# A decoder block on one core: the FFN's second product by seven half-size products, with weight sums made by DMA

## The chip, the core and the metric

The kernel runs on one core of one Trainium2 chip. A core has TensorE (PE, matmuls, with PEld for its weight loads), VectorE (DVE), ScalarE (ACT), GpSimd (POOL) and SyncE (SP, which here only issues DMAs), an on-chip memory SBUF of 128 partitions, a matmul accumulator PSUM of eight banks, and sixteen DMA engines to DRAM. The metric is the device time of one execution in microseconds, as the median of several runs; lower is better.

## The reference

One layer of a hybrid decoder: three mixers, their gated merge, an output projection, and a SwiGLU FFN, each half with an RMSNorm before and after and a residual. Batch 1, sequence S = 512, width D = 1024, FFN width DFF = 2816, all fp32. The changed part is the end:

```python
    x = x + rms_norm(merged @ w_out, norm_g[1])
    h = rms_norm(x, norm_g[2])
    gt, up = jnp.split(h @ w_ffn_in, 2, axis=-1)
    x = x + rms_norm((jax.nn.silu(gt) * up) @ w_ffn_out, norm_g[3])
```

## The kernel before

Every fp32 product is made of three fp32r matmuls (`mm3`, L119 to L122): high part by high part, high by low, low by high. A weight streams in as pieces of 128 x 1024 fp32 (512 KB): SP issues the load into `wraw` (three buffers), ACT casts it to `whi` (L92), and DVE or POOL subtracts to get `wlo` (L93); `whi` and `wlo` also have three buffers each. During the long projections a helper `take` keeps three pieces ahead of PE. The words "to split a tile" below mean these two operations, one on ACT and one on DVE or POOL.

The end of the kernel has three stages. The **front of the FFN** (L1176 to L1262): the output projection (w_out, eight pieces; 256 columns wide, so 384 matmuls of 256 columns) for token blocks 0 and 1 together and then 2 and 3 alone; behind each block `out_norm` (two squares on ACT, two multiplies by the gain on DVE, a reciprocal root, the residual `yf`, a square, another reciprocal root, `mix`), and `transpose_split` (L214 to L223), which turns `mix` by eight PE transposes and splits it into `hh` and `hl`. The first two column chunks of the FFN's first product go in `part` calls of 24 matmuls in that front, so that PE has work while the last blocks are normalised. The **first product** (`gemm_t`, L155 to L165) then goes chunk by chunk; `ffn_act` makes silu(gate) * up and splits it into `ah` and `al`. The **second product** (L1283 to L1331): 22 pieces of w_ffn_out, two passes of eleven (left and right half of the columns) into eight PSUM banks `acc`, four token blocks a pass, 24 matmuls of 512 columns for a piece, 528 in all. In the second pass the last three pieces are used block by block, so that a block's norm (square, gain, reciprocal root in `rstd_of`, residual, store) follows while PE is at the next block.

Each engine runs its own instructions in order. In this part of the kernel a scheduler has set that order. Splits in the FFN alternate between DVE and POOL (`cfg["lo"] = "vg"`, L1170).

## Time and profile before

| | us |
|---|---|
| median of three runs (range) | 1236.82 (1236.24 to 1239.58) |
| profiled execution | 1240.05 |
| its span in the trace | 1238.1 |
| PE busy in it | 1214.9 (98%) |
| DVE, ACT, POOL busy | 603.4, 526.7, 209.9 |
| front of the FFN, first w_out matmul to the first matmul of `gemm_t` | 815.21 to 892.07 |
| second product, first to last matmul | 1110.7 to 1230.3 |

An engine's busy time is the time in which it worked at something that the profiler records; the chain of waits follows the work that ended last back to the start. The page's own lines and the answers to queries on the trace stand in the section of rows below.

### The profile page before, as it was taken

What the parts mean: (1) busy time and instruction counts of PE and PEld (TensorE: products, weight loads), DVE (VectorE), ACT (ScalarE), POOL (GpSimd) and SP (SyncE); (2) the same over time, 40 slices, a digit from 0 to 9 for tenths busy, and PEclk for the clock granted to TensorE, in tenths of its full rate; (3) what the DMA queues carried; (4) which work ended last, traced back from release to release, by engine and by line L of the source; (5) the groups of instructions that cost most, each with busy time, mean ns of one, the idle gap of its engine ahead of it and who ended that gap; (6) DMA issues with size and microseconds to landing.
All of it is one profiled execution on the core that took longest, in us unless ns stands there. A gap on an engine that the chain in (4) does not pass through costs nothing.

```text
span 1238.1 us, 18045 instructions
## 1 busy us (share of the span) xinstructions
PE 1214.9 (98%) x7068; PEld 1032.8 (83%) x7068; DVE 603.4 (49%) x1275; ACT 526.7 (43%) x1008; POOL 209.9 (17%) x134
## 2 busy tenths in 40 slices
PE   8999999999999999999999999999999999999997
PEld 6887888787788888999998888898988888878886
DVE  6516657566576778465543343447433333331114
ACT  5335556665486676352432232334323222322222
POOL 1224544555000000000000000001122122221220
PEclk9998999999999999999999999999999999999999
DMA  7821422221233324223223343352233333322321
GB/s 254 236 73 36 88 70 65 65 65 52 67 104 96 94 68 108 83 70 82 73 69 102 92 145 121 102 171 69 58 97 102 102 99 89 102 90 98 94 94 68
DMA packets 152387, 117.99 MB, mean 95 GB/s; under 512 B 25106, under 2 KB 142078, under 8 KB 152304
## 3 DMA queue, kind: packets, MB, share of 16 engines
q1 hardware_dynamic: 151712, 115.81, 32.5%
q8 instruction: 55, 0.90, 0.3%
q10 hardware_dynamic: 592, 1.05, 0.2%
q14 instruction: 28, 0.23, 0.1%
HBM read 114.67 MB, written 2.17 MB: 94 GB/s over the span
## 4 chain that ended last, share of the span: by engine, by line
PE 90%; DVE 5%; ACT 3%; issue 1%; DMA 1%; SPq 0%; DVEq 0%; ACTq 0%
PE gps L797 17%; PE gps L162 13%; PE gps L800 9%; PE gps L120 7%; PE gps L165 7%; PE gps L121 7%; PE gps L122 7%; PE ops L650 3%; PE acc L120 3%; PE acc L121 3%; PE acc L122 3%; PE s L587 3%; PE ptp L627 2%; PE hid L426 1%; ACT p L598 1%
## 5 line engine op out<-in xcount | busy, mean ns | idle before, releaser
L92 ACT CAST whi<-wraw 128x1024 fp32r<-128x1024 f32 x177 | 185.0, 1050 | 350.3 <-PE gps L165 137.3
L93 DVE TENSOR_TENSOR wlo<-wraw,whi 128x1024 fp32r<-128x1024 f32 x122 | 148.9, 1228 | 242.6 <-ACT whi L92 165.8
L93 POOL TENSOR_TENSOR wlo<-wraw,whi 128x1024 fp32r<-128x1024 f32 x55 | 131.5, 2391 | 701.5 <-ACT whi L92 522.6
L162 PE MATMUL gps<-hh,whi 128*128 128x512 f32 x368 | 143.5, 390 | 0.0
L165 PE MATMUL gps<-hl,whi 128*128 128x512 f32 x368 | 143.4, 390 | 0.0
L797 PE MATMUL gps<-hh,whi 128*128 128x512 f32 x320 | 125.4, 392 | 1.5 <-ACT whi L92 1.5
L800 PE MATMUL gps<-hl,whi 128*128 128x512 f32 x320 | 124.6, 389 | 0.0
L605 POOL TENSOR_TENSOR p<-p,sc 128x256 f32<-128x256 f32 (+3 forms) x64 | 75.5, 1200 | 117.8 <-DVE sc L601 117.8
L120 PE MATMUL gps<-whi,hh 128*128 128x256 f32 x320 | 92.4, 289 | 0.0
L121 PE MATMUL gps<-wlo,hh 128*128 128x256 f32 x320 | 90.6, 283 | 1.5 <-DVE wlo L93 1.5
L162 PE MATMUL gps<-hh,wlo 128*128 128x512 f32 x368 | 90.9, 389 | 0.0
L122 PE MATMUL gps<-whi,hl 128*128 128x256 f32 x320 | 90.5, 283 | 0.0
L120 PE MATMUL gps<-hh,whi 128*128 128x512 f32 (+1 forms) x200 | 82.0, 415 | 3.4 <-ACT hh L222 1.5
L598 ACT ACTIVATE p<-p,mx 128x384 f32<-128x384 f32 (+3 forms) x128 | 68.7, 538 | 34.2 <-DVE mx L596 33.9
L162 PEld LDWEIGHTS gps<-hh,whi 128*128 128x128 f32 x368 | 69.1, 188 | 15.0 <-issue 0.9
L165 PEld LDWEIGHTS gps<-hl,whi 128*128 128x128 f32 x368 | 69.1, 188 | 14.5 <-issue 0.2
L162 PEld LDWEIGHTS gps<-hh,wlo 128*128 128x128 f32 x368 | 69.1, 188 | 14.4
L797 PE MATMUL gps<-hh,wlo 128*128 128x512 f32 x320 | 79.0, 389 | 0.0
L797 PE MATMUL gps<-yh,whi 128*128 128x512 f32 x192 | 74.9, 390 | 0.0
L800 PE MATMUL gps<-yl,whi 128*128 128x512 f32 x192 | 74.8, 389 | 0.0
L121 PE MATMUL gps<-hl,whi 128*128 128x512 f32 (+1 forms) x200 | 74.5, 374 | 0.0
L122 PE MATMUL gps<-hh,wlo 128*128 128x512 f32 (+1 forms) x200 | 74.2, 372 | 0.0
(314 smaller groups left out, 2401.9 us busy)
## 6 DMA issues: line engine op xcount, KB each, us to landing
wraw<-in_w_in_dram SPq DMA_DIRECT2D x60, 512.0 KB, 3.7
wraw<-in_w_ffn_in_dram SPq DMA_DIRECT2D x88, 256.0 KB, 3.2
wraw<-in_w_ffn_out_dram SPq DMA_DIRECT2D x22, 512.0 KB, 3.7
wraw<-in_w_in_dram SPq DMA_DIRECT2D x32, 256.0 KB, 3.2
wraw<-in_w_branch_dram SPq DMA_DIRECT2D x16, 512.0 KB, 3.3
bias<-line_d SPq DMA_DIRECT2D x16, 256.0 KB, 4.4
wraw<-in_w_in_dram SPq DMA_DIRECT2D x32, 128.0 KB, 2.7
wraw<-in_w_branch_dram SPq DMA_DIRECT2D x16, 256.0 KB, 4.4
```

Of the source, the lines that this page charges most:

```text
L92: a_.copy(hi, raw)
L93: lo_eng.tensor_tensor(lo, raw, f(hi), op=OP.subtract)
L120: pe.matmul(ps, lh, rh, start=first, stop=False)
L121: pe.matmul(ps, lh, rl, start=False, stop=False)
L122: pe.matmul(ps, ll, rh, start=False, stop=last)
L162: pe.matmul(ps[n], part_[:, k, c], ah[:, kk], start=kk == 0 and part_ is h, stop=kk == 7 and part_ is l)
L165: pe.matmul(ps[n], h[:, k, c], al[:, kk], start=False, stop=False)
L587: pe.matmul(s[gi][:, :n], q[h, qp, qs], kk[h, sl], start=i == 0, stop=i == 2)
L598: a_.activation(o, o, AF.Exp, scale=-1.0, bias=mx[:, br, gi:gi + 1], accum_out=sm[:, br, gi:gi + 1])
L605: g_.tensor_tensor(o, o, sc[:, br][:, :, None].to_broadcast([128, 2, n]), op=OP.mult)
L797: pe.matmul(ps[n], part_[:, k, c], ah[:, kk], start=kk == 0 and part_ is h, stop=kk == 7 and part_ is l)
L800: pe.matmul(ps[n], h[:, k, c], al[:, kk], start=False, stop=False)
```

## The change

**The second product.** The activations act (512 x 2816) and w_ffn_out (2816 x 1024) are cut in two in each dimension, and the four result quarters come from seven products of half size (p1 to p7) of sums and differences of quarters, instead of eight. A half-size product has 11 k steps (`NK`), two token tiles and three fp32r matmuls of 512 columns: 66 matmuls, 462 for seven. The first pass goes through k = 0 to 10 and uses two weight tiles at each: `tile_a` (two 256 KB loads) for p2 and p5, `tile_b` (one 256 KB load and a subtract on DVE) for p3 and p1. The second pass makes p4, p6 and p7 one after the other, six tiles each. So 40 tiles are split instead of 22, all on ACT and DVE. Each activation chunk pair becomes `ls` tiles by `first_sums`, `second_sums` and `split_ls`, and the result `C` lies in the old space of `hl`; adds and subtracts from the PSUM banks into C (`add`) are new. DVE, ACT and PE run this part in the order in which it is written.

**The weight sums.** Two tables in DRAM, `rows_d` and `cols_d`, hold sums of quarters of w_ffn_out. POOL issues 44 DMAs of 512 KB, DRAM to DRAM: 22 plain copies and 22 that accumulate onto them. Each follows a `tick`, a one-column copy on POOL that reads the `whi` tile of one of the pieces 12 to 55 of the projections, and so is paced by that stream.

**The front of the FFN.** w_out comes in pieces 512 columns wide (192 matmuls of 512 columns); the norms are cut in halves, those of blocks 0 and 1 run together; the pieces of the first two FFN chunks are split in the front and the `part` calls are all 256 tokens wide; the transposes (`turn`) stand at fixed places; x1 is also stored to DRAM (`x1_d`) and read back as `xr` before the last residual. POOL no longer splits FFN tiles.

The core of the diff:

```diff
+    def weight_sum(i, hi):
+        add, t, r, n, c0, c1, w = sums[i]
+        g_.tensor_copy(tick, f(hi[:, 0, 0:1]))
+        src = dap(w_ffn_out, r * D + (c1 if add else c0), [[D, n], [1, w]])
+        if add:
+            g_.dma_start(t[r:r + n], src, accum_op=OP.add, max_dma_last_dim=4096)
+        else:
+            g_.dma_start(t[r:r + n], src)
+
     def take():
         i = used[0]
         used[0] += 1
         while len(ready) < min(i + 3, len(pieces)):
-            ready.append(pieces[len(ready)]())
+            n = len(ready)
+            ready.append(pieces[n]())
+            if 12 <= n < 12 + len(sums):
+                weight_sum(n - 12, ready[n][0])
         return ready[i]
...
-    cfg["lo"] = "vg"
...
+        part(pss[0], fw[0], 0, t0, True, False)
+        turn(2)
+        s3 = norm_x((3,), s3)
+        norm_out((3,), s3)
+        part(pss[0], fw[1], 1, t0, False, False)
+        part(pss[1], fw[2], 0, t0, True, False)
+        part(pss[1], fw[3], 1, t0, False, False)
+        turn(3)
+        part(pss[0], fw[0], 0, t1, False, False)
...
+        def gain(tb, hf):
+
+            c = C[tb][:, hf * 512:hf * 512 + 512]
+            jk = fp.tile([128, 512], F32, name="fjk", tag="fsg", bufs=2)
+            a_.activation(jk, c, AF.Square, accum_out=ssf[:, tb, hf:hf + 1])
+            v_.tensor_tensor(c, c, gb3[:, hf * 512:hf * 512 + 512], op=OP.mult)
...
+            for k in range(NK):
+                w = weights()
+                use(p2, LS1[k], 1, w, 0, k)
+                use(p5, LS1[k], 2, w, 1, k)
...
+                w = weights()
+                use(p3, LS1[k], 3, w, 0, k)
+                use(p1, LS1[k], 0, w, 1, k)
...
+                if k:
+                    second(k - 1)
...
+            for p in range(NP - 3):
+                w = weights()
+                for k in range(2 * p, 2 * p + 2):
+                    use(p7, LS2[k], 1, w, k % 2, k)
+                if p in (0, 1):
+                    add(C[2 + p][:, c1], p6[p], C[2 + p][:, c1])
+                    gain(2 + p, 1)
+                    mean(2 + p)
+                if p == 1:
+                    root(2)
+                if p == 2:
+                    store(2, 0)
+                    store(2, 1)
+                    root(3)
+            w3 = [weights() for _ in range(3)]
+            for tt in range(2):
+                for k in range(2 * NP - 6, NK):
+                    use(p7, LS2[k], 1, w3[(k - 2 * NP + 6) // 2], k % 2, k, (tt,))
...
+            store(0, 0)
+            store(0, 1)
+            root(1)
+            store(1, 0)
+            store(1, 1)
```

`weights` takes the next split tile and has three split ahead (`ahead`); `mean` makes the mean square and its Sqrt on ACT, `root` the reciprocal and its correction on DVE, `store` the residual on DVE and the store of half a block, by ACT's queue for the left half and SP's for the right one.

**Order of ACT in the last product.** Before, behind the last pieces of the second pass (`whi_10520` to `whi_10532` are the last three; `fjk` is a block's square, `rs_r` its Sqrt):

```order
L92 CAST whi_10520<-wraw_10518 128x1024
L92 CAST whi_10526<-wraw_10524 128x1024
L92 CAST whi_10532<-wraw_10530 128x1024
L1307 ACTIVATE fjk_10554,ssf_9931<-acc10_9936 128x512
L202 ACT_TABLE_LOAD
L202 ACTIVATE rs_r_10562<-rs_m_10561 128x1
L1307 ACTIVATE fjk_10592,ssf_9931<-acc11_9937 128x512
```

After, in p7 (`whi_10633`, `whi_10662`, `whi_10696` and `whi_10723` are its third to sixth tile, the last of them half as wide):

```order
L1419 CAST whi_10633<-wraw_10630 128x1024
L1500 ACTIVATE fjk_10650,ssf_9815<-hl_9903 128x512
L1508 ACT_TABLE_LOAD
L1508 ACTIVATE rs_r_10656<-rs_m_10655 128x1
L1419 CAST whi_10662<-wraw_10659 128x1024
L1500 ACTIVATE fjk_10679,ssf_9815<-hl_9903 128x512
L1508 ACTIVATE rs_r_10685<-rs_m_10684 128x1
L1419 CAST whi_10696<-am_10693 128x1024
L1523 DMA out_0_dram<-hl_9903 128x512
L1419 CAST whi_10723<-am_10721 128x512
```

The squares and roots of blocks 2 and 3, which had stood behind the last split, now stand between the splits of the last three tiles.

**Order of DVE there.** Before, the last two subtracts and the first block's norm behind them (`fo` is the block's result):

```order
L93 TENSOR_TENSOR wlo_10521<-wraw_10518,whi_10520 128x1024
L93 TENSOR_TENSOR wlo_10533<-wraw_10530,whi_10532 128x1024
L1325 TENSOR_TENSOR fo_10557<-acc10_9936,gb3_9929 128x512
L1326 TENSOR_TENSOR ss3_10556<-ssf_9931 128x1
L201 TENSOR_SCALAR rs_m_10561<-ss3_10556 128x1
```

After, from the subtract of p7's fourth tile (`hl<-acc7` is the add of p6 into block 3, `rs_r_10656` block 2's root, `xr4` and `xr5` its residual):

```order
L1420 TENSOR_TENSOR wlo_10663<-wraw_10659,whi_10662 128x1024
L1551 TENSOR_TENSOR hl_9903<-acc7_9914,hl_9903 128x512
L1501 TENSOR_TENSOR hl_9903<-hl_9903,gb3_9813 128x512
L1505 TENSOR_TENSOR ss3_10682<-ssf_9815 128x1
L1507 TENSOR_SCALAR rs_m_10684<-ss3_10682 128x1
L1514 RECIPROCAL rs_r_10656<-rs_r_10656 128x1
L1515 SCALAR_TENSOR_TENSOR rs_t_10688<-rs_r_10656,rs_m_10655 128x1
L1516 TENSOR_SCALAR rs_t_10688<-rs_t_10688 128x1
L1517 TENSOR_TENSOR rs_r_10656<-rs_r_10656,rs_t_10688 128x1
L1420 TENSOR_TENSOR wlo_10697<-am_10693,whi_10696 128x1024
L1522 SCALAR_TENSOR_TENSOR hl_9903<-hl_9903,rs_r_10656,xr4_10492 128x512
L1522 SCALAR_TENSOR_TENSOR hl_9903<-hl_9903,rs_r_10656,xr5_10494 128x512
```

Block 3's add, gain and mean and block 2's root stand ahead of the fifth tile's subtract, and block 2's residual ahead of the sixth tile's.

**Order of POOL in the projections.** Before, POOL had little between the mixers' masks and the FFN (`p1`, `p2` are mixer tiles, `wlo_8311` belongs to the front of the FFN):

```order
L605 TENSOR_TENSOR p1_3673<-p1_3673,sc_3677 128x2x384
L605 TENSOR_TENSOR p2_3674<-p2_3674,sc_3677 128x768
L1117 AFFINE_SELECT cb_5008<-cb_5008 128x128
L1120 MEMSET at0_5009 128x512
L1120 MEMSET at1_5010 128x512
L93 TENSOR_TENSOR wlo_8311<-wraw_8307,whi_8310 128x1024
```

After, in the middle of the sums, where the plain copies end and the accumulating ones begin:

```order
L794 COPY tick_3871<-whi_5453 128x1
L799 DMA cols_d_101<-in_w_ffn_out_dram 256x512
L794 COPY tick_3871<-whi_5485 128x1
L799 DMA cols_d_101<-in_w_ffn_out_dram 256x512
L794 COPY tick_3871<-whi_5553 128x1
L797 DMA rows_d_100<-in_w_ffn_out_dram 128x1024
L794 COPY tick_3871<-whi_5611 128x1
L797 DMA rows_d_100<-in_w_ffn_out_dram 128x1024
```

A tick reads a `whi` buffer, so ACT's cast into that buffer, three pieces later, now waits for POOL to have come past that tick.

## Rows read from the trace of the kernel before

**Rows 1.** page: an engine's busy time and instructions; the chain of waits by engine
```profile
PE 1214.9 (98%) x7068; PEld 1032.8 (83%) x7068; DVE 603.4 (49%) x1275; ACT 526.7 (43%) x1008; POOL 209.9 (17%) x134
...
PE 90%; DVE 5%; ACT 3%; issue 1%; DMA 1%; SPq 0%; DVEq 0%; ACTq 0%
```

**Rows 2.** windows: busy time (count) of PE, PEld, DVE, ACT, POOL; clock, DMA, GB/s
```profile
650.00:700.00 50.00, 50.00 (x226) 41.52 (x225) 16.88 (x18) 13.98 (x17) 0.00 (x0) 1.00 0.33 95
...
1150.00:1200.00 50.00, 50.00 (x223) 41.39 (x222) 8.20 (x8) 12.36 (x18) 10.34 (x5) 1.00 0.32 97
```

**Rows 3.** tile `acc`: min/median/max ns, first and last start
```profile
L120 PE MATMUL acc<-whi,ah x176: 389/389/504, 1110.7 to 1229.9; 128*128 128x512 f32 x176
...
L122 PE MATMUL acc<-whi,al x176: 387/389/396, 1111.3 to 1230.3; 128*128 128x512 f32 x176
```

**Rows 4.** groups by line and form: busy, mean ns, idle before and releaser
```profile
L120 PE MATMUL acc<-whi,ah 128*128 128x512 f32 x176 | 68.6, 390 | 0.9 <-DVE fsg L1278 0.9
...
L92 ACT CAST whi<-wraw 128x1024 fp32r<-128x1024 f32 x177 | 185.0, 1050 | 350.3 <-PE gps L165 137.3 <-PE acc L122 79.2 <-PE gps L800 55.6
...
L93 DVE TENSOR_TENSOR wlo<-wraw,whi 128x1024 fp32r<-128x1024 f32 x122 | 148.9, 1228 | 242.6 <-ACT whi L92 165.8 <-PE gps L162 48.2 <-PE gps L797 23.2
...
L93 POOL TENSOR_TENSOR wlo<-wraw,whi 128x1024 fp32r<-128x1024 f32 x55 | 131.5, 2391 | 701.5 <-ACT whi L92 522.6 <-PE gps L162 177.4 <-DVE rs_r L203 1.5
...
L1215 DVE SCALAR_TENSOR_TENSOR yf<-mix,rs_r,yf 128x1024 f32<-128x1024 f32 x4 | 5.1, 1285 | 0.1
...
L1330 DVE SCALAR_TENSOR_TENSOR fo<-fo,rs_r,yf 128x512 f32<-128x512 f32 x8 | 5.7, 748 | 0.1
...
L202 ACT ACT_TABLE_LOAD x6 | 7.7, 1283 | 0.1
```

**Rows 5.** timeline of PE over the front of the FFN: start, length, instruction
```profile
815.21 0.28 PE L120 MATMUL gps<-whi,mth 128*128 128x256 f32 x1
...
861.18 1.03 PE L219 MATMUL tps<-ident,mix 128*128 128x128 f32 x8
...
863.49 0.61 PE L120 MATMUL gps<-hh,whi 128*128 128x256 f32 x3 [1.27 <-ACT hh L222]
...
865.20 0.38 PE L120 MATMUL gps<-hh,whi 128*128 128x256 f32 x1 [1.09 <-DVE mix L1211]
...
892.07 0.39 PE L162 MATMUL gps<-hh,whi 128*128 128x512 f32 x1
```

**Rows 6.** windows of the front: two around its longest PE wait
```profile
862.00:866.00 4.00, 1.42 (x8) 0.81 (x6) 3.59 (x9) 1.74 (x5) 0.00 (x0) 0.95 0.60 173
...
866.00:870.00 4.00, 4.00 (x24) 4.00 (x24) 2.40 (x9) 1.27 (x3) 0.00 (x0) 0.62 0.02 4
```

**Rows 7.** timeline of the end: PE, ACT and DVE
```profile
1230.31 0.39 PE L122 MATMUL acc<-whi,al 128*128 128x512 f32 x1
...
1230.80 0.60 ACT L1307 ACTIVATE fjk<-acc 128x512 f32<-128x512 f32 x1 [2.18 <-PE acc L122]
...
1231.52 0.69 DVE L1325 TENSOR_TENSOR fo<-acc,gb 128x512 f32<-128x512 f32 x1 [0.61 <-ACT fjk L1307]
...
1232.73 0.17 DVE L203 RECIPROCAL rs_r<-rs_r 128x1 f32<-128x1 f32 x1 [0.27 <-ACT rs_r L202]
...
1233.57 1.41 DVE L1330 SCALAR_TENSOR_TENSOR fo<-fo,rs_r,yf 128x512 f32<-128x512 f32 x2
```

**Rows 8.** page: SP's DMA queue; issues with us to landing
```profile
q1 hardware_dynamic: 151712, 115.81, 32.5%
...
wraw<-in_w_ffn_out_dram SPq DMA_DIRECT2D x22, 512.0 KB, 3.7
```

**Rows 9.** the w_out loads: a window, landing from 812 to 842, ACT
```profile
820.00:830.00 10.00, 10.00 (x88) 10.00 (x87) 5.76 (x6) 5.29 (x7) 0.00 (x0) 1.00 0.86 265
...
wraw<-in_w_out_dram SPq DMA_DIRECT2D x3, 512.0 KB, 5.1
...
828.92 1.05 ACT L1192 CAST woh<-wraw 128x1024 fp32r<-128x1024 f32 x1 [1.14 <-DMA wraw<-in_w_out_dram]
```

More of the change, by code (lines that the diff above doesn't have):

```diff
@@ L777, in hybrid_block_kernel @@
     used = [0]
+    sums = [(rows_d, r, 128, 0, 1408 * D, D) for r in range(0, 1408, 128)]
+    sums += [(cols_d, r, 256, 0, 512, 512) for r in range(0, DFF, 256)]
+    sums = [(add, *t) for add in (False, True) for t in sums]
+    tick = mp.tile([128, 1], F32, name="tick")
+    def weight_sum(i, hi):
[6 more added lines that the diff above has]
+            g_.dma_start(t[r:r + n], src)
     def take():
@@ L1240, in hybrid_block_kernel, with norm_half @@
-    transpose_split(mixes[2], 2, h2, pt, "pt")
-    def ffn_chunk(j):
-        return chunk(w_ffn_in, 0, 2 * DFF, [(j * 128, 128), (DFF + j * 128, 128)])
-    c0, c1 = ffn_chunk(0), ffn_chunk(1)
-    pss = [[pg.tile([128, S], F32, name="gps", tag="g") for _ in range(2)] for _ in range(2)]
-    def part(ps, ch, kh, t, first, last):
-        h, l = ch[kh]
+    def norm_half(tb, hf, ps):
+        if hf == 0:
+            mixes[tb] = xp_.tile([128, D], F32, name="mix", bufs=3)
+            ssms[tb] = xp_.tile([128, 2], F32, name="ssm", bufs=3)
+        jk = xp_.tile([128, 512], F32, name="mjk", bufs=1)
+        a_.activation(jk, ps, AF.Square, accum_out=ssms[tb][:, hf:hf + 1])
+        v_.tensor_tensor(mixes[tb][:, hf * 512:hf * 512 + 512], ps, gb1[:, hf * 512:hf * 512 + 512], op=OP.mult)
@@ L1252, in part, with ffn_piece @@
+    def ffn_piece(j, kh):
+        return [t.rearrange("p (k c) -> p k c", k=4) for t in split_w(ffn_raw(j, kh), v_)]
+    def part(ps, pc_, kh, t, first, last):
+        h, l = pc_
         for n in range(2):
@@ L1267, in hybrid_block_kernel, with ffn_chunk @@
+    def ffn_chunk(j):
+        return chunk(w_ffn_in, 0, 2 * DFF, [(j * 128, 128), (DFF + j * 128, 128)])
+    for tb in range(TB):
+        sy.dma_start(x1_d[:, tb], x1[:, tb])
     octx.close()
@@ L1269, in hybrid_block_kernel, with ls_tile, split_ls @@
     mo.__exit__(None, None, None)
+    yfc.__exit__(None, None, None)
     fp = ctx.enter_context(tc.tile_pool(name="ffn", bufs=1))
[L1271 to L1275 removed]
+    fr = ctx.enter_context(tc.tile_pool(name="ffr", bufs=1, side="right"))
+    LS1, LS2, raw2 = {}, {}, {}
+    def ls_tile():
+        return fp.tile([128, 2, 4, 256], F32R, name="ls", bufs=NK - 1)
+    def split_ls(t, src, n):
+        a_.copy(t[:, 0, :n], src)
+        v_.tensor_tensor(t[:, 1, :n], src, f(t[:, 0, :n]), op=OP.subtract)
@@ new lines, in split_u, with wsrc, tile_a @@
+    def split_u(raw, n=1024):
+        hi = wpool.tile([128, 1024], F32R, name="whi")
+        lw = wpool.tile([128, 1024], F32R, name="wlo")
+        a_.copy(hi[:, :n], raw[:, :n])
+        v_.tensor_tensor(lw[:, :n], raw[:, :n], f(hi[:, :n]), op=OP.subtract)
+        return hi, lw
+    def wsrc(r, c):
+        return dap(w_ffn_out, r * 128 * D + c * 512, [[D, 128], [1, 512]])
+    last = {}
+    def tile_a(k):
+        t = last["a"] = raw_tile()
+        sy.dma_start(t[:, 0:512], wsrc(k, 0))
+        sy.dma_start(t[:, 512:1024], wsrc(NK + k, 1))
+        return split_u(t)
@@ new lines, in tile_b, with pair, load @@
+    def tile_b(k):
+        t, ab = raw_tile(), last["a"]
+        sy.dma_start(t[:, 0:512], rows_d[k * 128:k * 128 + 128, 512:1024])
+        v_.tensor_tensor(t[:, 512:1024], ab[:, 0:512], ab[:, 512:1024], op=OP.subtract)
+        return split_u(t)
+    def pair(src):
+        def load(p):
+            t = raw_tile()
+            n = min(2, NK - 2 * p)
+            for i in range(n):
+                sy.dma_start(t[:, i * 512:i * 512 + 512], src(2 * p + i))
+            return split_u(t, n * 512)
+        return load
@@ new lines, in hybrid_block_kernel, with ahead, weights @@
+    NP = (NK + 1) // 2
+    stream = [(fn, k) for k in range(NK) for fn in (tile_a, tile_b)]
+    for src in (lambda k: rows_d[k * 128:k * 128 + 128, 0:512], lambda k: cols_d[k * 128:k * 128 + 128],
+                lambda k: cols_d[(NK + k) * 128:(NK + k) * 128 + 128]):
+        stream += [(pair(src), p) for p in range(NP)]
+    done = []
+    turns = [0]
+    def ahead(n):
+        while len(done) < min(n, len(stream)):
+            fn, k = stream[len(done)]
+            done.append(fn(k))
+    def weights():
+        i = turns[0]
+        turns[0] += 1
+        ahead(i + 3)
+        return done[i]
```

309 lines of the change are left out of this document (209 added, 100 removed).

## The prediction

> **What bounds the kernel now.** First the page: PE is busy for 98% of the span, and the chain of waits runs through PE for 90% of it [rows 1]. What counts is therefore PE's instructions and the places where PE waits. Next the stages. In two windows, one in the projections and one in the second product, PE is busy for every microsecond at full clock, while DVE, ACT and POOL are busy for a third or less [rows 2]. The second product starts at 1110.7 and its last matmul at 1230.3 [rows 3], so one 512-column matmul follows the other every (1230.3 − 1110.7) / 527 = 0.227 us; the 0.39 us of a row is the pipelined length. Its only wait is 0.9 us at its first matmul [rows 4]. The front of the FFN is where PE loses time: 815.21 to 892.07 is 76.86 us [rows 5], with waits of 1.27 and 1.09 us there, after which the granted clock of the next 4 us reads 0.62 [rows 6]. Last the tail: the last matmul starts at 1230.31 and the last residual ends at 1233.57 + 1.41 = 1234.98 [rows 7].
>
> **The second product: fewer matmuls.** 528 − 462 = 66 matmuls × 0.227 = **−15.0 us** [rows 3]. The wait of 0.9 us at the boundary also goes: the first k step uses p2 and p5 in other banks than those that the last chunk still holds, and p3, which needs them, comes 12 matmuls (2.7 us) later, against 1.3 us for silu and multiply: **−0.9**.
>
> What each k step needs beside PE is hidden. A step is 24 matmuls, 5.44 us. ACT has two casts of 1.05 us and the cast of a `ls` tile, about 2.9 us; DVE has two subtracts of 1.23, half a tile for `tile_b` (0.69) and one `ls` subtract, about 4.1 us [rows 4]. POOL's subtract of 2.39 us is no longer used there. In p4 DVE's adds join the splits: it has 4.9 and 4.0 us of work in the first two tiles, which last 2.72 us each (12 matmuls), and falls 3.5 us behind, but it is two tiles (5.4 us) ahead. So this is costed at nothing; if DVE were ahead by less than 3.5 us, the difference would stand on PE.
>
> Weights: a 512 KB load took 3.7 us in this product [rows 8]. A tile of the second pass is consumed in 2.72 us and its raw buffer is asked for two to three tiles ahead. Stepping through the queue of raw buffers, I find that a landing of up to 5 us costs nothing, 7 us 2.4, 8 us 4.5 and 10 us 15. Near the w_out loads the DMA engines were 0.86 busy at 265 GB/s, loads of 512 KB landed in 5.1 us, and ACT once waited 1.14 us for one [rows 9]; p4 to p7 ask for 512 KB in 2.72 us, 193 GB/s. I take 0 and keep +4.5 for the range.
>
> **A new wait in p7.** Before, the squares and roots of blocks 2 and 3 stood behind the last split. Now they stand between the splits of the last three tiles, and engines run in order. Count from p7's first matmul. PE takes 2.72 us for each of the first three tiles, then the fourth, fifth and sixth for one token tile (1.36, 1.36 and 0.68), then again for the other. It wants the fifth tile at 8.16 + 1.36 = 9.52.
> On ACT: block 2's square is done at 3.9 (it waits for the add of p6, 0.69 [rows 7], and for the third tile's subtract ahead of it on DVE), a table load of 1.28 ends at 5.1 and the Sqrt at 5.25, so the fourth tile's cast ends only at 6.2 and its subtract at 7.5. Block 3's add stands behind that subtract: 7.4 to 8.1. Its square, 0.72 from its start to DVE's next step (1230.80 to 1231.52), ends at 8.9, the gain on DVE at 9.5, the mean at 9.85, the Sqrt at 10.05. Only then does ACT cast the fifth tile, to 11.0: PE waits 1.5 us, and its second matmul waits 1.0 more for the subtract (to 12.3). DVE then has block 2's residual, two of 0.748 (1.41 as a pair), and block 3's root (0.85, from the reciprocal to the residual, 1232.73 to 1233.57) before the sixth tile's subtract: wanted at 13.66, there at 15.06, 1.4 us late [rows 4, 7]. Sum **+4.0 us**. Nothing in the trace of before has this wait; the bounds are 0, if the order between the engines leaves more room than this walk has, and the +4.0.
>
> **The tail.** Before, 1230.31 to 1234.98 is 4.67 us. After it there is one add more behind the last matmul (0.69), and block 0's two residuals (1.41, of which some 0.3 lies beside the Sqrt of block 1) stand ahead of block 1's root on DVE: 0.69 + 1.1 = **+1.8 us** [rows 7].
>
> **The front.** Before: w_out's 384 matmuls and one group of eight transposes (1.03) fill the 45.97 us from 815.21 to 861.18, 0.117 for a matmul of 256 columns [rows 5]. Then come the `part` calls (144 matmuls of 256 columns, at about 0.120, and 24 of 512, 22.7 us) and three groups of transposes (3.1). The rest of the 76.86, 5.1 us, is lost: 2.8 us of waits (the two shown and two short ones) and so 2.3 of slow clock. After: 192 matmuls × 0.227 = 43.6, four transposes 4.1, eight `part` calls of 24 × 0.120 = 23.0, sum 70.7. Waits: following DVE's queue, block 3's chain there ends (`hl` of block 2, then 6.4 us for root, residual of 1.285, square, root, `mix` of 1.285 [rows 4]) about 0.6 us after PE wants to transpose it, and the copies behind the transposes add 0.3 and 0.6, w_out's fifth subtract 0.2: 1.8. Sum 72.5, **−4.3 us**. The bounds are 0 (the old losses come back) and −6.1 (no wait at all).
>
> **Clock.** In the front of before, a stretch in which PE worked for 1.42 us of 4 was followed by one at a granted clock of 0.62 [rows 6]. Between the two levels (1.2 and 2.4 GHz) that is mostly the lower one. The new front has waits of 1.5 us close together and p7 some 2.6 in 2.8. I take **+1.0 us**, between 0 and the 2.3 that the fall in the front of before cost.
>
> **The weight sums.** They lie in the projections, roughly from 440 to 680 us, and move 23.07 MB beside loads that take a third of the DMA engines there [rows 2]. Price of a byte: 115.81 MB took 32.5% of the 1238.1 us span [rows 8], 402 us, 288 GB/s. 23.07 MB are 80 us, or 120 us if an accumulating byte counts twice, over some 235 us: 0.34 to 0.51 beside 0.33, below 1. The loads there have slack: three raw buffers at 5.44 us a piece, less a landing near 3.7, are over 12 us. The Trainium skill ("DMA: Bandwidth & Descriptors", section "Issuing engines are not separate DMA queues") says that a DMA issued by POOL runs on the same sixteen engines as those of SP. It speaks against taking these sums as free; by it the shares add as they have just been added from rows, and the sum stays 0; no row of before has a large DMA from POOL to show it.
>
> The other price is POOL's own. A tick waits behind the DMA issue ahead of it, and ACT's cast three pieces on waits for the tick. A piece lasts 24 matmuls, 5.44 us, and the stream is two pieces, 10.9 us, ahead. So POOL may take 5.44 + 10.9 / 44 = 5.69 us for a DMA before PE waits; beyond, the loss is 44 × (x − 5.44) − 10.9. No row shows x. The nearest is POOL's dearest operation, 2.39 us [rows 4]; on the upper side 512 KB at the share that is left free (two thirds of 288 GB/s, two bytes moved for one) are 5.8 us. I take the nearest row, **0 us**. The same page, section "Anatomy of one DMA", gives 2.0 us plus bytes at 436 GB/s for a DMA from POOL, an estimate of 3.2 us; by it, too, the sum stays 0. No run here shows it.
>
> **Sum.** −15.0 − 0.9 + 4.0 + 1.8 − 4.3 + 1.0 = −13.4 us. The profiled execution took 1240.05, 3.2 above the median of 1236.82; by the median, 1223.4.
>
> **Rivals.**
> *The wait in p7 is not there.* For it: before's tail hides its norms well, and the chip may run ACT ahead of my walk. Against it: ACT's order is fixed. 1219.
> *Weights late in the second product.* 18 more tiles and two small loads for most of them. For it: the 5.1 us of the w_out loads [rows 9], at my limit of 5. Against: 3.7 us in this product. Landing at 8 us gives 1228, at 10 us 1238.
> *It comes to nothing.* The front gives nothing (+4.3), the weights land in 8 us (+4.5), and the clock costs 1.3 more: 1223.4 + 10.1 = 1233.5, within 0.3% (3.7 us, about what a measurement of this kernel tells from no change).
> *Slower: POOL holds the stream.* The accumulating DMAs read two operands and write one; should POOL need x us for each issue or the queue behind it, the loss is 44 × (x − 5.44) − 10.9. It decides from 5.69 us; the kernel is slower by over 0.3% from x = 6.1; at 6.5 us the loss is 35.7 and the time 1259. For it: no large POOL DMA in the trace, and the 5.8 us above lies near the threshold. Against: the head start, and eight DMAs in flight, 8 × 5.44 = 43.5 us for each to finish.
>
> **How the numbers follow.** Forecast (1220 to 1226) 0.56; no wait in p7 0.13; weights late 0.14, of which some 0.02 ends within 0.3%; nothing 0.07; POOL holds the stream 0.10, of which 0.01 stays within 0.3% or below. Faster 0.81, same 0.10, slower 0.09. The range from 1217 to 1231 leaves out the slow rival, nothing-case and the worst of the late weights, a little under 0.2.
>
> **What would show it.** Right: 462 `acc` matmuls at 0.227 us; PE waits of 1 to 1.5 us for the fifth and sixth tiles of p7, put down to ACT's and DVE's splits; the front's 76.86 at about 72.5; PE without idle time between 440 and 680 us. Wrong: PE idle in the projections with ACT's `whi` waiting for POOL (the slow rival); `acc` matmuls that wait for a `wraw` load (late weights); p7 without waits (1219); a granted clock below 1 in more than a few microseconds around the new waits, which would make my 1.0 too small.

## The result and the profile after

The changed kernel takes 1226.89 us in the median against 1237.27 for the kernel before, measured together; the ratio is 0.9907 with a 95% interval of 0.9894 to 0.9921. One of its six executions took 1591.24 us at a granted clock of 0.70; it is among the six of the median, and the ratio leaves it out. The profiled execution took 1227.31 us with a span of 1225.3. The prediction has two footings: from the profiled execution of before, 1240.05 − 13.4 = 1226.65, which was met within 0.7 us; and by the median, 1223.4, of which 1226.89 is 3.5 us above. So the median lies inside the range of 1217 to 1231, and 0.9 us above the narrower one of 1220 to 1226.

The page after, first PE's busy time and the chain of waits by engine, which answer to [rows 1]; then the queue of POOL's DMAs and the issues of the weight sums, which are new; then the loads of w_ffn_out in the second product, which answer to [rows 8]:

```profile
PE 1201.0 (98%) x6834; PEld 1012.8 (83%) x6834; DVE 674.9 (55%) x1378; ACT 554.8 (45%) x1040; POOL 186.0 (15%) x189
...
PE 90%; DVE 5%; ACT 3%; issue 1%; DMA 1%; DVEq 0%; SPq 0%; ACTq 0%
...
q0 software_dynamic: 6512, 23.07, 8.5%
...
rows_d<-in_w_ffn_out_dram POOLq DMA_DIRECT2D x22, 512.0 KB, 5.3
cols_d<-in_w_ffn_out_dram POOLq DMA_DIRECT2D x22, 512.0 KB, 6.0
...
wraw<-in_w_ffn_out_dram SPq DMA_DIRECT2D x18, 256.0 KB, 3.3
```

PE still is the bound: 13.9 us less of it, 12.8 us less of span. Stage by stage, from PE's timelines of both kernels:

| stage | before, us | after, us | difference |
|---|---|---|---|
| up to the first w_out matmul | 815.21 | 814.72 | −0.5 |
| front, to the first matmul of the first product | 76.86 | 73.08 | −3.8 |
| first product, to the first `acc` matmul | 218.6 | 218.6 | 0.0 |
| second product, first to last `acc` matmul | 119.6 | 109.1 | −10.5 |
| last matmul's start to the end of the span | 7.8 | 9.7 | +1.9 |

PE's timeline after, from the first w_out matmul to the first of the first product, answers to [rows 5]:

```profile
814.72 0.39 PE L120 MATMUL gps<-whi,mth 128*128 128x512 f32 x1
...
852.68 0.55 PE L219 MATMUL tps<-ident,mix 128*128 128x128 f32 x3 [0.26 <-DVE hl L223]
...
875.73 0.38 PE L120 MATMUL gps<-hh,fw 128*128 128x256 f32 x1 [0.24 <-ACT hh L222]
876.45 0.39 PE L121 MATMUL gps<-hl,fw 128*128 128x256 f32 x1 [0.34 <-DVE hl L223]
...
887.80 0.40 PE L162 MATMUL gps<-hh,whi 128*128 128x512 f32 x1
```

Three short waits are left of the front's losses (0.26, 0.24 and 0.34 us), and no stretch at a lower clock follows them: in windows from 848 to 888 us the granted clock is 1.00 throughout.

PE's timeline where the second product begins, at the fifth tile of p7, and at its last matmul:

```profile
1106.44 0.50 PE L120 MATMUL acc<-whi,ls 128*128 128x512 f32 x1 [0.85 <-DVE am L1393]
...
1207.57 0.50 PE L120 MATMUL acc<-whi,ls 128*128 128x512 f32 x1 [1.52 <-ACT whi L1419]
...
1208.83 0.79 PE L121 MATMUL acc<-wlo,ls 128*128 128x512 f32 x1 [0.76 <-DVE wlo L1420]
...
1209.42 0.63 PE L122 MATMUL acc<-whi,ls 128*128 128x512 f32 x1
...
1211.13 0.63 PE L120 MATMUL acc<-whi,hh 128*128 128x512 f32 x1
...
1215.56 0.39 PE L122 MATMUL acc<-whi,hh 128*128 128x512 f32 x1
```

The boundary wait of 0.85 us is still there. The fifth tile's first matmul waits 1.52 us for ACT's cast and its second 0.76 for DVE's subtract (starts 1207.57 and 1208.83, so it comes 1.03 us later than the beat of 0.227 would have it). Then the matmuls come every 0.43 us until about 1212, and the sixth tile's (the `hh` rows, from 1211.13) show no wait.

The windows there (length, busy time and count of PE, PEld, DVE, ACT and POOL, granted clock, DMA share, GB/s):

```profile
1206.00:1209.00 3.00, 0.72 (x3) 0.36 (x3) 2.32 (x9) 1.18 (x2) 0.00 (x0) 0.96 0.00 0
1209.00:1212.00 3.00, 3.00 (x7) 2.15 (x8) 2.90 (x8) 0.62 (x1) 0.00 (x0) 0.50 0.45 175
```

In the 3 us in which PE works for 0.72 us the clock is still 0.96; in the next 3 it is 0.50, the lower of the two levels (1.2 of 2.4 GHz), although PE is busy throughout.

ACT's timeline there:

```profile
1204.59 0.63 ACT L1500 ACTIVATE fjk<-hl 128x512 f32<-128x512 f32 x1 [1.89 <-DVE hl L1551]
...
1206.33 0.20 ACT L1508 ACTIVATE rs_r<-rs_m 128x1 f32<-128x1 f32 x1 [1.02 <-DVE rs_m L1507]
1206.47 1.04 ACT L1419 CAST whi<-am 128x1024 fp32r<-128x1024 f32 x1
```

The square of block 3 waits for DVE's add, the Sqrt for DVE's mean, and the fifth tile's cast (1206.47) stands behind both. The last residual on DVE's timeline, which answers to the last line of [rows 7]:

```profile
1220.55 1.41 DVE L1522 SCALAR_TENSOR_TENSOR hl<-hl,rs_r,xr 128x512 f32<-128x512 f32 x2
```

It ends at 1221.96, 6.40 us after the last matmul's start, against 4.67 before.

### The profile page after: what moved, and what is told of

Same layout as the page of the kernel before. It is cut to its first block, busy times and chain, and to the rows that moved or that the text cites. A ratio compares the mean times of both kernels' runs of the same rounds, so it can differ in the third digit from the quotient of the medians.

```text
span 1225.3 us, 18001 instructions
## 1 busy us (share of the span) xinstructions
PE 1201.0 (98%) x6834; PEld 1012.8 (83%) x6834; DVE 674.9 (55%) x1378; ACT 554.8 (45%) x1040; POOL 186.0 (15%) x189
## 4 chain that ended last, share of the span: by engine, by line
PE 90%; DVE 5%; ACT 3%; issue 1%; DMA 1%; DVEq 0%; SPq 0%; ACTq 0%
PE gps L822 17%; PE gps L162 14%; PE gps L825 9%; PE gps L120 7%; PE gps L121 7%; PE gps L122 7%; PE gps L165 7%; PE ops L656 3%; PE s L593 3%; PE acc L121 3%; PE acc L122 3%; PE acc L120 3%; PE ptp L633 2%; PE hid L432 1%; ACT p L604 1%
## 5 line engine op out<-in xcount | busy, mean ns | idle before, releaser
L92 ACT CAST whi<-wraw 128x1024 fp32r<-128x1024 f32 x153 | 159.6, 1049 | 248.8 <-issue 94.9
L93 DVE TENSOR_TENSOR wlo<-wraw,whi 128x1024 fp32r<-128x1024 f32 x131 | 159.0, 1221 | 147.4 <-ACT whi L92 111.9
L162 PEld LDWEIGHTS gps<-hh,whi 128*128 128x128 f32 x368 | 69.1, 188 | 15.0 <-issue 0.9
L165 PEld LDWEIGHTS gps<-hl,whi 128*128 128x128 f32 x368 | 69.1, 188 | 14.5 <-issue 0.2
L162 PEld LDWEIGHTS gps<-hh,wlo 128*128 128x128 f32 x368 | 69.1, 188 | 14.3
L120 PE MATMUL gps<-hh,whi 128*128 128x512 f32 (+1 forms) x176 | 74.2, 423 | 0.8 <-DVE hl L304 0.8
L822 PEld LDWEIGHTS gps<-hh,whi 128*128 128x128 f32 x320 | 60.1, 188 | 14.5 <-ACT whi L92 2.0
L825 PEld LDWEIGHTS gps<-hl,whi 128*128 128x128 f32 x320 | 60.1, 188 | 12.5
L822 PEld LDWEIGHTS gps<-hh,wlo 128*128 128x128 f32 x320 | 60.1, 188 | 12.5
```

Of the source, the lines that this page charges most:

```text
L92: a_.copy(hi, raw)
L93: lo_eng.tensor_tensor(lo, raw, f(hi), op=OP.subtract)
L120: pe.matmul(ps, lh, rh, start=first, stop=False)
L162: pe.matmul(ps[n], part_[:, k, c], ah[:, kk], start=kk == 0 and part_ is h, stop=kk == 7 and part_ is l)
L165: pe.matmul(ps[n], h[:, k, c], al[:, kk], start=False, stop=False)
L822: pe.matmul(ps[n], part_[:, k, c], ah[:, kk], start=kk == 0 and part_ is h, stop=kk == 7 and part_ is l)
```

## The experiments

The stage lengths below are from each kernel's own trace. They are steadier than whole times: between traces the part ahead of w_out differs by 2 to 3 us with the same instructions (see the last section), so a whole time is compared as a ratio to the kernel before on the same chip.

### The changed kernel again

The same code, so that its variants have a companion.

> The changed kernel again, so that it and its variants stand on one chip. Theory: the ratio of its first measurement, 0.9907, within 0.0015; stage by stage the same lengths as in its first trace (front 73.1 us, first to last matmul of the second product 109.2, from there to the end 9.7). The early part, up to the first w_out matmul, may differ by 2 to 3 us with the granted clock between 80 and 100 us, as it did between kernels with the same early instructions. Rival (its first trace was a poor execution and the stages themselves vary): stages differ by over 0.5 us.

Measured: 1225.14 us, ratio 0.9903 (0.9882 to 0.9925). In the trace the first w_out matmul comes at 814.6, the first and last `acc` matmul at 1106.3 and 1215.4, and the span ends at 1225.1: 109.1 us for the second product and 9.7 behind it, as in the first trace. The theory holds: for the changed kernel stages can be compared to a tenth or two. For the kernel before they can not all be: see the front in the weight sums alone.

### The norms behind the splits

```diff
-                if p in (0, 1):
-                    add(C[2 + p][:, c1], p6[p], C[2 + p][:, c1])
-                    gain(2 + p, 1)
-                    mean(2 + p)
-                if p == 1:
-                    root(2)
-                if p == 2:
-                    store(2, 0)
-                    store(2, 1)
-                    root(3)
+                if p == 0:
+                    for q in (0, 1):
+                        add(C[2 + q][:, c1], p6[q], C[2 + q][:, c1])
+                        gain(2 + q, 1)
+                if p == 1:
+                    mean(2)
+                    mean(3)
             w3 = [weights() for _ in range(3)]
+            root(2)
+            store(2, 0)
+            store(2, 1)
+            root(3)
```

> The changed kernel with one edit: in the seventh product the reciprocal roots, residuals and stores of blocks 2 and 3 stand behind the split of its last tile instead of between the splits of the last three. Theory (one queue of DVE work, so that a wait removed ahead of the last matmul comes back behind it): PE's waits in the seventh product fall from 2.7 us (1.7 and 1.0) to about 1.6, the last matmul is about 2.4 us earlier counted from the product's start (the clock's fall included, 2.9), and the tail from the last matmul to the last residual grows from 6.4 to about 8.1 us; net gain 0.6 to 1.1 us against the changed kernel, so some 1226 us in the median. Rival (the wait is worth what it shows): the waits and the slow clock behind them, 4.4 us in all, are gained, and the tail stays at 6.4: about 1222.5 us.

Measured: 1224.76 us, ratio 0.9877 (0.9862 to 0.9892). By stages: 106.2 us for the second product (2.9 less than the changed kernel, as the theory had it), 11.3 from the last matmul to the end (1.6 more): 1.3 us net. PE's timeline at the fifth tile:

```profile
1205.99 0.50 PE L120 MATMUL acc<-whi,ls 128*128 128x512 f32 x1 [0.26 <-ACT whi L1419]
1207.25 0.51 PE L121 MATMUL acc<-wlo,ls 128*128 128x512 f32 x1 [0.76 <-DVE wlo L1420]
```

And DVE's behind it, where the residual of block 2 (from 1208.55) is followed by that of block 3 and then block 0's add:

```profile
1210.71 1.42 DVE L1522 SCALAR_TENSOR_TENSOR hl<-hl,rs_r,xr 128x512 f32<-128x512 f32 x2
1212.04 0.68 DVE L1551 TENSOR_TENSOR hl<-acc,hl 128x512 f32<-128x512 f32 x1
```

The waits are smaller and no slow matmuls follow them, but DVE now has the residuals of blocks 2 and 3 up to 1212.04. PE starts block 0's last matmul at 1208.95, 15 intervals of 0.227 before its last one at 1212.36, and is through with it 0.4 us later; block 0's add starts 2.7 us behind that, and all that follows with it. The theory's direction holds and its size (0.6 to 1.1) was a little low; the rival's 4.4 us with an unchanged tail is excluded: what a shorter PE gains there, DVE's queue takes back in part.

### The walked order

The same instructions of PE, ACT and DVE, in an order found from the walk through the queues; beside the order, the stores of the left halves go by SP's queue instead of ACT's, all but the last. The core:

```diff
+            for q in (2, 3):
+                add(C[q][:, c1], p6[q - 2], C[q][:, c1])
+            ahead(n7 + 3)
+            square(2, 1)
+            p7_pair(0)
+            mul(2, 1)
+            p7_pair(1)
+            half_mean(2)
+            square(3, 1)
+            half_mean(3)
+            mul(3, 1)
+            sqrt(2)
+            root(2)
+            p7_pair(2)
+            ahead(n7 + 4)
+            sqrt(3)
+            ahead(n7 + 5)
+            root(3)
+            store(2, 0)
+            ahead(n7 + 6)
+            store(2, 1)
+            store(3, 1)
+            p7_end(0)
+            add(C[0][:, c0], p7[0], C[0][:, c0])
+            store(3, 0)
+            square(0, 0)
+            half_mean(0)
+            sqrt(0)
+            p7_end(1)
+            mul(0, 0)
+            root(0)
+            add(C[1][:, c0], p7[1], C[1][:, c0])
+            square(1, 0)
+            store(0, 1)
+            store(0, 0)
...
```

> The changed kernel with the order of ACT and DVE in the seventh product and behind it written anew, from a walk through their queues with the measured durations: adds and squares of blocks 2 and 3 ahead of or between the first splits, no residual ahead of the last split's subtract except one, block 0's root and residuals in the time in which DVE waits for ACT, all stores but the last by SP's queue. The same instructions on PE, ACT and DVE. Theory: PE has no wait in the seventh product and the clock stays at full, so its 30 matmuls behind the third tile take 6.8 us instead of 9.9; the tail is 5.5 us instead of 6.4; gain 4 us from the order of before the tail and 0.8 in it, some 5 us together, about 1222 us in the median. Rival (DVE's work sets the end whatever its order): PE ends earlier, the tail grows by as much, gain under 2 us, 1225 or more.

Measured: 1220.05 us, ratio 0.9842 (0.9829 to 0.9856). PE has no wait in the seventh product; from the first to the last `acc` matmul it is 104.6 us, which is 461 intervals of 0.227, and 8.8 us follow, 0.9 less than in the changed kernel. Together 5.4 us by stages, against 5 expected. PE's first and last `acc` matmul, and DVE behind the last:

```profile
1103.65 0.50 PE L120 MATMUL acc<-whi,ls 128*128 128x512 f32 x1 [0.85 <-DVE am L1393]
...
1208.27 0.39 PE L122 MATMUL acc<-whi,hh 128*128 128x512 f32 x1
...
1209.31 1.41 DVE L1602 SCALAR_TENSOR_TENSOR hl<-hl,rs_r,xr 128x512 f32<-128x512 f32 x2
...
1212.32 1.41 DVE L1602 SCALAR_TENSOR_TENSOR hl<-hl,rs_r,xr 128x512 f32<-128x512 f32 x2
```

Block 0's two residuals (1209.31, 1.41 us) now lie in the time in which DVE waits for block 1's square; the last residual ends 5.46 us after the last matmul's start. That DVE's total work sets the end (the rival) is excluded: DVE was busy for 674.3 us, 674.9 in the changed kernel, and 5.4 us went by the order (with the stores' queue, which was not tried by itself).

### The waits filled with work

```diff
+                    if tt == 0 and k == 8:
+                        ls, (wh, wl) = LS2[k], [x[:, 0:512] for x in w3[1]]
+                        h, l = ls[:, 0, 1, 0:128], ls[:, 1, 1, 0:128]
+                        for _ in range(7):
+                            pe.matmul(p1[0], h, w3[0][0][:, 0:512], start=True, stop=True)
+                        pe.matmul(p7[0], h, wh, start=False, stop=False)
+                        for _ in range(5):
+                            pe.matmul(p1[0], h, w3[0][0][:, 0:512], start=True, stop=True)
...
```

> The changed kernel with twelve extra matmuls in the two waits of the seventh product's fifth tile, seven ahead of its first matmul and five behind it, into a bank that nothing reads; so PE waits as long, but works meanwhile. It asks what the slow clock behind the waits costs by itself. Theory: the clock stays at full, the matmuls behind come every 0.227 us instead of 0.43, and the 1.65 us of slow clock go; but PE then meets the sixth tile's subtract, which ends as late as before, and waits about 1.2 us there; net 0.4 us earlier at the last matmul. Rival 1 (clock and waits add up): 1.6 us earlier, no wait for the sixth tile. Rival 2 (the clock falls for another reason than PE's idle time): matmuls at 0.43 us as before.

Measured, one execution: 1226.17 us. PE's timeline at the fifth and sixth tile:

```profile
1205.06 1.75 PE L1601 MATMUL acc<-whi,ls 128*128 128x512 f32 x7
...
1209.81 0.50 PE L120 MATMUL acc<-whi,hh 128*128 128x512 f32 x1 [0.28 <-ACT whi L1419]
1210.66 0.50 PE L121 MATMUL acc<-wlo,hh 128*128 128x512 f32 x1 [0.34 <-DVE wlo L1420]
```

And its windows, with the columns as above:

```profile
1206.00:1209.00 3.00, 3.00 (x14) 2.23 (x13) 2.44 (x4) 0.69 (x1) 0.00 (x0) 1.00 0.00 0
1209.00:1212.00 3.00, 2.38 (x10) 1.42 (x9) 2.90 (x9) 0.62 (x1) 0.00 (x0) 1.00 0.45 175
```

The clock stays at 1.00, and the fifth tile's last matmuls come every 0.23 us. But PE meets the sixth tile earlier and now waits there: its first two matmuls start 0.43 and 0.62 us beyond the beat. From the first to the last `acc` matmul it is 1105.6 to 1214.4, 108.8 us, 0.3 less than the 109.1 of the changed kernel. So the slow clock cost about 0.3 us, not the 1.65 that the matmuls' spacing shows: behind it lay the sixth tile's subtract, which ends when it ends (rival 1 is excluded).

Why the clock fell in the changed kernel stays open, and rival 2 is not excluded. The trace of the double pace (below), whose seventh product has the changed kernel's code, has the same two waits of the fifth tile, with nothing to fill them. Its PE timeline and windows there:

```profile
1213.69 0.49 PE L120 MATMUL acc<-whi,ls 128*128 128x512 f32 x1 [1.51 <-ACT whi L1420]
1214.94 0.50 PE L121 MATMUL acc<-wlo,ls 128*128 128x512 f32 x1 [0.77 <-DVE wlo L1421]
...
1216.76 0.50 PE L120 MATMUL acc<-whi,hh 128*128 128x512 f32 x1 [0.39 <-ACT whi L1420]
...
1212.00:1215.00 3.00, 0.72 (x3) 0.24 (x2) 2.32 (x9) 1.18 (x2) 0.00 (x0) 1.00 0.00 0
1215.00:1218.00 3.00, 2.27 (x8) 1.35 (x9) 2.90 (x8) 0.62 (x1) 0.00 (x0) 1.00 0.45 175
```

PE again works for 0.72 of 3 us, and the clock stays at 1.00. So the idle time came before the fall in the changed kernel, in both of its traces, but it does not always bring one, and the full clock of the filled run does not show that the filling kept it. The price is confirmed: here, too, PE waits for the sixth tile instead (0.55 and 0.61 us beyond the beat), and the first `acc` matmul at 1112.56 and the last at 1221.36 are 108.8 us apart.

### The accumulators in the open pools

On top of the walked order:

```diff
-        psum_ctx.close()
...
-        with tc.tile_pool(name="facc", bufs=1, space=PSUM) as fa:
-            acc = [fa.tile([128, 512], F32, name=f"acc{i}") for i in range(8)]
-            p3, p1, p2, p5 = [acc[2 * i:2 * i + 2] for i in range(4)]
+        with psum_ctx:
+            p2, p5, p3, p1 = [[pool.tile([128, 512], F32, name="acc", tag=tag) for _ in range(2)]
+                              for pool, tag in ((pa, "a"), (pt, "pt"), (pg, "g"), (pg, "g"))]
```

> The kernel with the walked order of the end, and one more edit: the accumulators of the second product are taken from the PSUM pools that are already open instead of from a new pool over all eight banks, so that each waits only for the last reader of its own bank; p2 and p5 get banks that the last chunk of the first product does not hold. Theory (the 0.85 us at the first accumulating matmul, which the prediction had put to nothing and which is still there, is the release of the whole old pool): the wait goes, the second product starts 0.85 us earlier and the whole is 0.9 us shorter than the walked order alone, some 1219 us or ratio 0.0007 lower, which the trace shows and the times hardly can. Rival (the wait is for the operands, the first split tiles or the last activations): it stays at 0.85.

Measured: 1218.98 us, ratio 0.9849 (0.9831 to 0.9868), on the chip on which the changed kernel has 0.9903: 6.2 us less in the medians. PE's timeline at the boundary:

```profile
1101.68 1.98 PE L162 MATMUL gps<-hh,wlo 128*128 128x512 f32 x8
1103.49 0.39 PE L120 MATMUL acc<-whi,ls 128*128 128x512 f32 x1
```

Eight matmuls of the first product begin at 1101.68 and the first `acc` matmul follows on the beat, 8 × 0.227 = 1.82 us later. The wait was for PSUM, not for the operands. That it was for the old pool as a whole and not for one bank is not separated by this run, but the first bank in use was `acc00` before and `acc4`, the fifth in the list of its eight, after, and both waited for the last chunk's multiply. By stages this is the shortest version of the study: 404.0 us from the first w_out matmul to the end of the span, 405.1 in the walked order; the whole times of the two can't be told apart.

### The front alone

The kernel before with the new front and nothing else of the change (the diff is that of the front, with the chunks in their old order).

> The kernel before with only the new front of the FFN (w_out in pieces of 512 columns, norms in halves, fixed places of the transposes); the second product as before, no weight sums. Theory (the front's gain is its own): the stretch from the first w_out matmul to the first matmul of the first product falls from 76.9 us to about 73.1, as in the changed kernel, and the whole by the same 3.8 us: about 1233.5 us against 1237.3, ratio 0.997. Rival (the gain needs the earlier part, or the second product gives it back): ratio 0.999 or more.

Measured: 1233.74 us, ratio 0.9957 (0.9944 to 0.9969). Its front takes 73.23 us (73.08 in the changed kernel, 76.86 before), the second product 119.6 as before. The front's gain is its own and stays (its size is taken up again in the next experiment). The ratio lies below the expected 0.997, but the profiled execution also reached w_out 2.8 us earlier than before's, with the same instructions there.

### The weight sums alone

The kernel before with the `weight_sum` part of the change; nothing reads the sums.

> The kernel before with only the 44 weight-sum DMAs of POOL added, at the changed kernel's pace; nothing reads the sums. Theory (hidden): no wait of PE in the projections, landing of the weight loads beside them grows from 3.6 us to as much as 7.8 and is covered by the three raw buffers; time within 0.3% of before, 1237 plus or minus 2. Rival (they cost something that the changed kernel's other gains cover up): 2 us or more above before, with PE idle between 430 and 690 us or at a lower granted clock there.

Measured: 1238.4 us, ratio 0.9999 (0.9988 to 1.0009). The stretch from 560 to 700 us as a window, in the kernel before:

```profile
560.00:700.00 140.00, 140.00 (x828) 125.18 (x828) 62.15 (x117) 46.67 (x68) 0.00 (x0) 1.00 0.30 83
```

In the changed kernel:

```profile
560.00:700.00 140.00, 140.00 (x828) 125.20 (x827) 61.78 (x115) 46.78 (x67) 23.93 (x36) 1.00 0.69 152
```

In this one:

```profile
560.00:700.00 140.00, 140.00 (x829) 125.18 (x828) 60.86 (x112) 45.67 (x66) 28.63 (x34) 1.00 0.69 154
```

PE is busy for all 140 us in each, and from 430 to 560 us, where the other sums lie, for 128.2 of 130 in each. The DMA share goes from 0.30 to about 0.69, POOL's busy time from nothing to 24 and 29 us, and landings of 512 KB loads of `w_in` between 560 and 680 from 3.6 us to 4.4 here and 7.8 in the changed kernel; none of it reaches PE. No cost of the sums shows at this pace, and the interval allows for no more than 1.1 us.

The front of this run is before's code in a second trace, and it is 75.31 us long (812.58 to 887.89), not 76.86. Its two longest waits of PE and the window behind them, which answer to [rows 5] and [rows 6]:

```profile
860.78 0.62 PE L120 MATMUL gps<-hh,whi 128*128 128x256 f32 x3 [1.19 <-ACT hh L222]
...
862.49 0.39 PE L120 MATMUL gps<-hh,whi 128*128 128x256 f32 x1 [1.08 <-DVE mix L1230]
...
863.00:867.00 4.00, 3.91 (x33) 3.92 (x34) 3.35 (x11) 1.26 (x3) 0.00 (x0) 1.00 0.02 7
```

The waits are those of [rows 5] to a tenth, but the clock behind them is 1.00 and not 0.62. So 1.5 us of the 3.8 that the front gained are a slow stretch in before's own trace, which its code does not always have.

### Twice the pace

```diff
-            if 12 <= n < 12 + len(sums):
-                weight_sum(n - 12, ready[n][0])
+            if 12 <= n < 12 + len(sums) // 2:
+                weight_sum(2 * n - 24, ready[n][0])
+                weight_sum(2 * n - 23, ready[n][0])
```

> The changed kernel with two weight sums behind each of 22 pieces instead of one behind each of 44: the same DMAs in half the stretch. It asks how near the rival of the prediction was (POOL holds the stream). Theory: POOL takes up to 2.2 us for a tick and an issue, 4.4 us for two, under the 5.44 us of a piece, so POOL holds nothing; the DMA engines carry 0.30 of their time for the loads and 0.35 for the sums at the present pace, so 1.0 at the double one, landings pass 12 us and PE waits for late weights: 2 to 10 us lost, all of it between 430 and 570 us, put down to loads. Rival 1 (slack holds): no PE wait, 0 us. Rival 2 (POOL is the limit): PE waits for splits whose cast waits for POOL, with POOL busy or waiting on its DMA queue throughout.

Measured: 1233.41 us, ratio 0.9983 (0.9961 to 1.0004), 8.3 us above the median of the changed kernel again. The first w_out matmul comes at 820.8, 6.2 us after the changed kernel's; but this trace has a granted clock of 1.00 between 80 and 100 us, as the walked order has, whose code is the same up to there and which comes to w_out at 812.0. Against that, 8.9 us are lost. ACT's waits for loads of `w_in` over the whole trace (us in total, times, the longest):

```profile
ACT whi L92 <- DMA wraw<-in_w_in_dram: 46.6, 13, 5.9
```

PE's longest wait in the stretch, from its timeline:

```profile
501.28 1.65 PE L1078 MATMUL itps<-qt,ee 128*128 128x192 f32 x4 [5.31 <-DVE at L1072]
```

And two windows:

```profile
490.00:500.00 10.00, 5.96 (x50) 5.70 (x48) 4.09 (x12) 2.77 (x4) 3.48 (x5) 1.00 1.08 246
500.00:510.00 10.00, 8.72 (x50) 8.73 (x51) 4.72 (x10) 1.35 (x2) 5.47 (x8) 0.66 1.11 231
```

The DMA share is above 1, the 512 KB loads issued between 430 and 520 land in a median of 16.6 us (4.6 in the changed kernel), ACT's casts wait for loads 13 times, 46.6 us in all (3 times and 8.3 us in the changed kernel), and behind a late subtract on DVE stands the `at` tile for which PE waits 5.31 us, with the clock at 0.66 in the next window. POOL was busy for 28.2 of the 70 us from 430 to 500. Its ticks wait for ACT's casts, and no cast is put down to a tick. So the resource that gives out first is the DMA engines, at twice the pace, and not POOL; the theory holds, with the one difference that PE's wait is put down to DVE, one step behind the load.

## Why the prediction was right, and where it was not

**Fewer matmuls, −15.0.** Right. 462 `acc` matmuls at 0.227 us; without waits (the walked order) first to last takes 104.6 us, against 119.6 before: 15.0.

**The boundary, −0.9.** Wrong. The step said that p2 and p5 use other banks than the last chunk and so need not wait. The first `acc` matmul still waited 0.85 us for that chunk's last multiply; with banks of the open pools it did not. The wait in [rows 4] had the same releaser, and the prediction read it as the wait of one bank, where the new pool lies over all eight; which of the two PE waits for is not separated.

**The wait in p7, +4.0.** Right, in place, mechanism and size. ACT's cast was 1.5 us late as walked and DVE's subtract 1.0. The third part, 1.4 us for the sixth tile, was walked at full clock, and shows where the clock stays full: in the double pace's trace the sixth tile's two matmuls come 1.16 us late together, and the second product is 4.2 us longer than without waits. (The three parts of the walk make 3.9.)

**The clock, +1.0.** The mis-sized term: 0.3 us in p7, nothing in the front. In the changed kernel PE was slow for about 4 us behind the fifth tile, so it came later to the sixth and met it ready; the stage lost 4.5 us (10.5 gained instead of 15.0), 0.3 more than at full clock. The prediction added the slow clock to the waits, and they overlap. It also took [rows 6] as what follows a wait; in the sums-alone trace the same waits had no slow stretch behind them.

**The tail, +1.8.** Right: 4.67 to 6.40, +1.7.

**The front, −4.3.** Right in sign; −3.8 between the two profiled executions, and −2.2 against the other trace of before's front (75.31), which has no slow stretch. On the length after, 72.5 forecast and 73.08 measured, two errors partly cancel. The w_out term was mis-sized: 192 × 0.227 = 43.6 took the beat of the second product, but w_out's matmuls of 512 columns come every 0.2333 us (814.72 to 816.59 is eight of them), 44.8 us, exactly what 384 of 256 columns took (0.1167 each). Halving their number gave nothing, where −1.3 was booked. Against that the waits were smaller: 0.84 us in the three rows, where 1.8 was booked (its parts make 1.7); the transposition of block 3 did not wait. Some 0.3 us are left that no row explains.

**The sums, 0.** Right, and the rival is far off. POOL's price, which the prediction bounded between 2.39 and 5.8 us, is a tick of 0.23 us in the middle (1.33 at most) and an issue of 0.49 to 0.89, under 2.3 us; by the prediction's sum PE would wait from 5.69. The upper bound was miscounted: two bytes moved for each of 512 KB at two thirds of 288 GB/s are 5.5 us, under that threshold, not 5.8 above it. All ticks (shortest, middle and longest in ns, first and last start; the first comes earlier than the 440 us of the prediction):

```profile
L794 POOL COPY tick<-whi x44: 175/233/1331, 392.7 to 667.4; 128x1 f32<-128x1 f32 x44
```

On the DMA engines the sums took 8.5% of the span, 104 us, between the 80 and 120 of the prediction. POOL's queue from 440 to 525 us, when it makes plain copies, and from 535 to 675, when it accumulates (packets, MB, share of the engines' time):

```profile
q0 software_dynamic: 1677, 7.34, 26.5%
...
q0 software_dynamic: 4426, 11.00, 47.9%
```

That is 326 GB/s of engine time while it copies and 164 while it accumulates, so a byte cost twice as much there; its packets were also smaller, 2.5 KB against 4.4, and which of the two it was is not separated.

The Trainium skill, "DMA: Bandwidth & Descriptors", section "Anatomy of one DMA", gives a fixed time plus one by size, by which the prediction had an estimate of 3.2 us for 512 KB; here the landings have a median of 5.3 and 6.0 us, beside loads on the same engines, so the measurement decides, and it is longer. The trace agrees with the same page of the Trainium skill, section "Issuing engines are not separate DMA queues", by which the DMAs of POOL and SP share their engines: the loads' landing rose from 3.6 to 7.8 us, and at twice the pace they came too late.

**Weights in the second product, 0.** Right: PE waits for no load there; the 256 KB loads of w_ffn_out land in 3.3 us, under the 5 that the prediction took as the limit.

**The other 0.5.** The part ahead of w_out was 0.5 us shorter for no reason of the change; its clock differed between the executions.

So the profiled time came within 0.7 us in part by luck: terms that were too favourable (the boundary 0.9, the front 0.5, p7 0.2) stood beside the clock, booked 0.7 too high, and those 0.5 us. The pair of executions was lucky, too: before's has the slow stretch in the front and the slowest early part of the traces. The medians differ by 10.4 us, and the ratios of the two rounds (0.9907 and 0.9903) stand for 11.5 and 12.0, against 13.4 forecast. The main terms, 66 matmuls fewer, the wait in p7 and the tail, came out within 0.2 us each.

## What to carry to other kernels

Write out the queue of each engine around the last few tiles and walk it with measured durations: it gave a wait of 2.5 us that no row of before showed, and then an order that takes 5.4 us off with the same instructions. Losses in a row (a wait, the slow clock behind it, the next wait) are not a sum: give each the start that the one ahead leaves it. Take a matmul's beat from its own stage, not from another of the same shape. Read the same stage in a second trace before a slow stretch in it is booked as something to gain. And take accumulators from pools that are open if only some of the banks must be free.

## What the runs showed of the hardware that was not expected

The granted clock early in the kernel differs between traces with the same instructions there. The window from 80 to 100 us, in the kernel before:

```profile
80.00:100.00 20.00, 19.12 (x101) 16.17 (x100) 7.95 (x30) 9.00 (x23) 4.05 (x3) 0.85 0.19 53
```

In the changed kernel:

```profile
80.00:100.00 20.00, 19.12 (x105) 16.13 (x105) 7.37 (x28) 9.01 (x23) 4.63 (x2) 0.91 0.19 53
```

In the walked order:

```profile
80.00:100.00 20.00, 19.12 (x112) 16.34 (x111) 8.12 (x30) 9.01 (x23) 4.45 (x4) 1.00 0.20 53
```

PE is busy for the same 19.12 us of the 20, but the clock is 0.85, 0.91 and 1.00, and w_out begins at 815.2, 814.7 and 812.0. The changed kernel has 0.91 in both of its traces, so these windows alone do not tell executions from kernels; but the executions of one kernel differ as much in the whole (the weight sums alone took from 1236.39 us at a mean clock of 0.998 to 1240.90 at 0.993). That is up to 3 us of a change of 10, so a ratio between two single executions can be off by 0.25% for that alone, and stages measured from one mark to another are the better comparison.

The clock behind PE's waits is no more regular: twice, in the front of before and in p7, the same code with the same waits to a tenth of a microsecond had a slow stretch behind them in one trace (0.62 and 0.50) and none in another. What decides it stays open.

Matmuls of one shape (128 x 128 by 512 columns) have a beat of 0.227 us in the second product and of 0.2333 in w_out, each at a granted clock of 1.00; between 837 and 848 us, where the DMA share is 0.24, w_out's is still 0.233. What makes the difference was not tried and stays open.
